# A two-layer decoder trunk: output-weight sums loaded ahead and stored in one go, the last two products exchanged, score groups joined

## The chip, the cores and the metric

The kernel runs on one core of one Trainium2 chip. The metric is the device time of one execution in microseconds, lower is better. Before the change the median of three executions is 1103.44 us (1101.58 to 1105.78). A profiled execution of its own took 1101.21 us; its span, from the first to the last instruction, is 1099.5 us.

## The reference

The input is 1024 tokens of 1024 float32 numbers. Two layers follow.

```python
# layer 1: gated MLP with a causal mixing of tokens inside chunks of 128
u, v, z = split(rms_norm(h) @ w_in, 3)            # 1024 x 2048 each
v = layer_norm(gelu(v))
s = einsum('gts,bnsgc->bntgc', tril(w_s), v) + b_s   # 8 groups of 256 channels
h = h + rms_norm((gelu(u) * s * silu(z)) @ w_out)
k, v = rms_norm(h) @ w_k, rms_norm(h) @ w_v          # 4 heads of 64, shared
# layer 2: attention over a window of 128 keys, 16 query heads, ALiBi, one sink per head
q, z = split(rms_norm(h) @ w_in, 2)
p = softmax([q k^T / 8 + alibi, sink])               # the sink only enters the sum
h = h + rms_norm((p v * silu(z)) @ w_out)
```

## The kernel before

Every large matrix product is done to nearly float32 precision in three matmuls. Each operand is split into a rounded part *hi* and a rest *lo* (`split`: ScalarE writes hi with a copy, L105, VectorE writes lo by a subtraction, L106), and `mm3` (L203 to L205) adds hi x hi, hi x lo and lo x hi into one bank. On top of this the products of a two-by-two block matrix are done in seven products in place of eight (the Winograd form of Strassen's scheme), numbered 1 to 7. It needs sums and differences of the blocks of either operand, and sums of the products.

The stages, in order: `v_layer` (v), `uz_layer` (u and z, the token mixing, the gate), `out_layer` (the first output product and its norm), query and gate products, keys and values, and attention, into which the remaining products are filled, ending with the output product of layer 2 (`Out.early`, `Out.late`).

**uz_layer** goes over 16 *quads*: eight channel groups g, each first for u (zz = 0), then for z (zz = 1). A quad does products 1, 2, 6, 5, 7 of its own and products 4 and 3 of the quad before. Products 1, 6 and 7 add into one bank (tile `ub` in the profile): after each, ScalarE copies the running sum out (`copy`, L243), and the next product adds on. Products 5 and 3 use the bank `uc`, product 2 uses `ua`. `prep1` to `prep3` make the split weights a product or two ahead (GpSimd makes the sums `f`, L240). Gelu (L724) and silu (L654) stand on ScalarE and each needs its function table loaded. `normalise` (L638) works on the group's part of v (`vg`), which `group_consts` loads; `spatial` does the mixing.

**presum** is a generator that uz_layer steps six times a quad (`step(sums_b)`). It has nothing to do with that stage: it makes the sums of the layer-2 output weights `wo_b` that the seven products at the end need, in 16 pieces of 128 columns, splits them, and stores hi and lo to DRAM (`od`). Piece by piece, before the change: four loads, five additions on GpSimd, four splits, eight stores, three splits, six stores. All seven blocks of a piece lie in one tile `presum`, of which the lo parts overwrite the sums, so the next piece's loads go into what the last piece's stores read.

**The order of the work.** The program is traced in Python's order, and a scheduler with a cost model then orders each engine's instructions by priority and by when it takes their inputs to be there. `tc.keep_in_program_order` pins an instruction behind the one traced last on its engine. On the chip each engine works off its list in order; DMAs that SyncE (SP) issues stand in one such list too, and each waits there for what it needs.

**Weights** (class `Weights`) hands out split weight pairs through `wnext`. The first 20 are split on the spot; later ones are read back from DRAM by `back`, among them the output weights in the order 4, 2, 5, 1, 7, 6, 3, two halves u each, into a ring of three pairs (`o_ring`).

**Attention** runs 16 units (a block of 128 queries and a pair of key heads). `ORDER` gives the parts of a step: 0 and 1 are the two score groups, a and b their exponentials, n and m their normalising, t the transposes of the unit before, v, g and p values, gate and split of the one before that, F a piece of the filling products. Scores, transposes and values share four banks with the tag "s". VectorE reduces the scores (L1134, L1141).

**The end.** `Out.early` does products 4, 2, 5, 1, 7 for 512 tokens in four blocks t; `final` (L1281) applies the root of the norm and adds the residual, and stores to the output (L1282). `Out.late` does product 6 into banks of its own and then product 3 (`og`), and adds the latter to two sums. Each block then has two squares on ScalarE (L1319), two scalings, the root on GpSimd (L1275) and two final passes.

## Time and profile before

| | before |
|---|---|
| median of three executions | 1103.44 us |
| profiled execution, its span | 1101.21 us, 1099.5 us |
| TensorE busy | 1043.5 us (95%) |
| VectorE, ScalarE, GpSimd busy | 780.2, 546.0, 266.0 us |
| mean granted TensorE clock | 0.975 |
| uz_layer, first to last product | about 162 to 541 us |

Columns of a row of the page: line, engine, operation, output tile and input tiles, sizes, count. PE is TensorE, PEld its weight loads, DVE VectorE, ACT ScalarE, POOL GpSimd, SPq the DMA list of SyncE. A timeline row has the start, the duration, and in brackets how long the engine was idle before it and who released it. Matmuls overlap: a row says 0.39 us, but they follow each other 0.227 us apart, so the distance of starts is what counts.

### The profile page before, as it was taken

The numbers are of one execution on the slowest core, as the hardware profiler recorded it, in microseconds if no ns is written. First come the engines' busy times: TensorE is split into PE (matmuls) and PEld (weight loads), VectorE is DVE, ScalarE is ACT, GpSimd is POOL, SyncE is SP. The second block draws the span as 40 slices with busy tenths as digits, with TensorE's granted clock in tenths as the row PEclk, the third lists the DMA queues.
The fourth block names the chain that finished last, engine by engine and source line by source line (L and its number), as shares of the span: only waits on it lengthen the run. The fifth ranks groups of instructions, "written<-read, shape, count | busy, mean of one in ns | idle before, by whom it ended". The sixth has DMA issues, their size and how long they took to land.

```text
span 1099.5 us, 15046 instructions
## 1 busy us (share of the span) xinstructions
PE 1043.5 (95%) x5186; PEld 848.7 (77%) x5186; DVE 780.2 (71%) x1374; ACT 546.0 (50%) x1046; POOL 266.0 (24%) x260
## 2 busy tenths in 40 slices
PE   9999999899889898899999999999999999998983
PEld 7887888787668687787888888888987777776772
DVE  6988377859667697867778668555166667778565
ACT  6684255555545556555444556444044445454322
POOL 0000023365353635353100000000001113144324
PEclk9999999999989999999999999999999999999896
DMA  8786245655545454555898652997145334344472
GB/s 305 261 284 251 96 153 159 182 161 164 157 154 154 142 168 152 171 160 173 300 358 309 232 181 89 325 350 249 58 159 194 137 135 145 124 148 156 170 270 110
DMA packets 130285, 210.17 MB, mean 191 GB/s; under 512 B 11681, under 2 KB 71969, under 8 KB 130209
## 3 DMA queue, kind: packets, MB, share of 16 engines
q1 hardware_dynamic: 125696, 200.53, 53.9%
q10 hardware_dynamic: 4512, 8.68, 2.2%
q8 instruction: 41, 0.67, 0.3%
q14 instruction: 36, 0.29, 0.1%
HBM read 144.15 MB, written 65.01 MB: 190 GB/s over the span
## 4 chain that ended last, share of the span: by engine, by line
PE 63%; DVE 13%; DMA 9%; POOL 6%; ACT 4%; issue 3%; SPq 2%; DVEq 0%; POOLq 0%; ACTq 0%
PE qz L203 6%; PE qz L204 5%; PE qz L205 5%; DVE uz_slots L240 4%; PE ob L205 3%; PE ob L203 3%; PE oc L203 3%; PE ob L204 3%; PE oc L204 3%; PE oc L205 3%; POOL presum L240 3%; PE vb L204 2%; PE vb L205 2%; DMA presum<-in_wo_b_dram 2%; DMA od<-presum 2%
## 5 line engine op out<-in xcount | busy, mean ns | idle before, releaser
L1147 ACT ACTIVATE pr<-pr,mx 128x129 f32<-128x129 f32 x128 | 50.4, 395 | 70.9 <-DVE mx L1141 70.9
L203 PE MATMUL ub<-T,uzhilo_g 128*128 128x512 f32 x128 | 55.6, 434 | 25.8 <-ACT uz_slots L243 25.8
L203 PE MATMUL qz<-n_hi,whi_w 128*128 128x512 f32 x192 | 77.4, 403 | 0.0
L204 PE MATMUL qz<-n_lo,whi_w 128*128 128x512 f32 x192 | 75.0, 391 | 0.0
L205 PE MATMUL qz<-n_hi,wlo_w 128*128 128x512 f32 x192 | 74.9, 390 | 0.0
L105 ACT ACTIVATE presum<-presum 128x128 fp32r<-128x128 f32 x112 | 31.4, 305 | 85.4 <-POOL presum L240 52.6
L106 DVE TENSOR_TENSOR presum<-presum 128x128 fp32r<-128x128 f32 x112 | 41.5, 408 | 42.4 <-POOL presum L240 34.5
L110 DVE SCALAR_TENSOR_TENSOR wlo_w<-raw_w,gn,whi_w 128x512 fp32r<-128x512 f32 x40 | 28.7, 748 | 48.4 <-ACT whi_w L109 48.4
L109 ACT ACTIVATE whi_w<-raw_w,gn 128x512 fp32r<-128x512 f32 x40 | 27.1, 716 | 62.9 <-PE pv L205 30.4
L203 PE MATMUL ub<-T,whi_g 128*128 128x512 f32 x128 | 51.9, 406 | 2.4 <-ACT uz_slots L243 2.4
L204 PE MATMUL ub<-T,uzhilo_g 128*128 128x512 f32 x128 | 53.4, 417 | 0.0
L205 PE MATMUL ub<-T,uzhilo_g 128*128 128x512 f32 x128 | 53.4, 417 | 0.0
L203 PEld LDWEIGHTS ub<-T,uzhilo_g 128*128 128x128 f32 x128 | 26.2, 204 | 34.4 <-ACT uz_slots L243 29.2
L1167 POOL TENSOR_SCALAR_AFFINE_SELECT pc<-pc 128x1024 f32<-128x1024 f32 x16 | 21.4, 1336 | 121.7 <-DVE dn L1153 109.6
L205 PE MATMUL ub<-T,wlo_g 128*128 128x512 f32 x128 | 50.7, 396 | 0.0
L204 PE MATMUL ub<-T,whi_g 128*128 128x512 f32 x128 | 50.6, 395 | 0.0
L240 POOL TENSOR_TENSOR presum<-presum 128x128 f32<-128x128 f32 x80 | 38.9, 517 | 46.9 <-DMA presum<-in_wo_b_dram 38.6
L106 DVE TENSOR_TENSOR uzhilo_g<-f,uzhilo_g 128x1024 fp32r<-128x1024 f32 x31 | 43.8, 1414 | 7.8 <-ACT uzhilo_g L105 7.3
L203 PE MATMUL uc<-T,uzhilo_g 128*128 128x512 f32 x124 | 48.9, 395 | 0.0
L204 PE MATMUL uc<-T,uzhilo_g 128*128 128x512 f32 x124 | 48.3, 389 | 0.0
L205 PE MATMUL uc<-T,uzhilo_g 128*128 128x512 f32 x124 | 48.3, 389 | 0.0
L240 POOL TENSOR_TENSOR f<-raw_uz 128x512 f32<-128x512 f32 x15 | 20.1, 1338 | 112.5 <-DMA raw_uz<-in_wuz_in_dram 96.3
(400 smaller groups left out, 3332.0 us busy)
## 6 DMA issues: line engine op xcount, KB each, us to landing
raw_uz<-in_wuz_in_dram SPq DMA_DIRECT2D x32, 512.0 KB, 3.9
od<-presum SPq DMA_DIRECT2D x224, 64.0 KB, 1.9
td<-uz_slots SPq DMA_DIRECT2D x56, 256.0 KB, 2.1
orawP2a<-td SPq DMA_DIRECT2D x28, 512.0 KB, 4.2
raw<-in_wv_in_dram SPq DMA_DIRECT2D x17, 512.0 KB, 4.7
vg<-vd SPq DMA_DIRECT2D x8, 1024.0 KB, 6.4
orawP2b<-in_wo_a_dram SPq DMA_DIRECT2D x16, 512.0 KB, 7.7
raw_w<-in_wqz_dram SPq DMA_DIRECT2D x16, 512.0 KB, 5.2
```

Source lines behind the costliest of these rows:

```text
L105: nc.scalar.activation(hi, src, AF.Copy)
L106: nc.vector.tensor_tensor(lo, src, hi.bitcast(F32), ALU.subtract)
L109: nc.scalar.activation(hi, src, AF.Copy, scale=g)
L110: nc.vector.scalar_tensor_tensor(lo, src, g, hi.bitcast(F32), ALU.mult, ALU.subtract)
L203: nc.tensor.matmul(out, lhsT=a_hi, rhs=b_hi, start=start, stop=False, skip_group_check=True)
L204: nc.tensor.matmul(out, lhsT=a_hi, rhs=b_lo, start=False, stop=False, skip_group_check=True)
L205: nc.tensor.matmul(out, lhsT=a_lo, rhs=b_hi, start=False, stop=stop, skip_group_check=True)
L240: (eng or nc.vector).tensor_tensor(out, a, b, op)
L1147: nc.scalar.activation(pr[:, i], pr[:, i], AF.Exp, bias=mx[:, i:i + 1], scale=-1.0, accum_out=dn[:, i:i + 1])
L1167: nc.gpsimd.affine_select(pc, pc, [[0, 8], [1, P]], ALU.is_ge, 0.0, base=0, channel_multiplier=-1)
```

## The change

- *presum*: a piece's four blocks come with two loads into a tile of their own (tag "junk"), and the loads of the next piece are put out right after the sums of this one. The five sums go from the raw blocks into five tiles `lo`, pinned in program order on GpSimd; five splits follow, pinned on ScalarE and VectorE; one DMA then stores all ten tiles. Blocks m = 4 and m = 3, which are plain blocks of the weights and no sums, are no longer made here.
- *Weights*: halves of m = 4 and m = 3 are loaded raw one pair ahead and split when their pair is fetched (`early_raw`, `back`). Product 3 now comes before product 6.
- *uz_layer*: `load_consts(g + 1)` moves behind `normalise(g)`, and the masking of `wc` on GpSimd becomes `mask_consts`, called in the z quad.
- *Attention*: `ORDER` has 0 and 1 next to each other. In the last four units the difference that product 3 needs stays where it is made and is what `post` splits; the sum for product 6 is split in `late`.
- *The end*: `late` does product 3 first and then product 6 on top of it in the same banks (after the block's sum with product 3 alone is read out). The second half's scaling goes to VectorE, into another tile; the root's first part is made for four blocks at once. The output stores of blocks 0 and 1 of the first half are put out after the last weights have been asked for.

```diff
-            self.order += [(None, f"o{m}{u}") for m in (4, 2, 5, 1, 7, 6, 3) for u in range(2)]
+            self.order += [({4: wo_b[1, u], 3: wo_b[0, 2 + u]}.get(m), f"o{m}{u}")
+                           for m in (4, 2, 5, 1, 7, 3, 6) for u in range(2)]
...
         def back(self, i):
             for n in range(20 + len(self.ready), i + 1):
                 self.ready[n] = (w_ring if n < 36 else o_ring).take(f"w{n}")
+                if self.order[n][0] is not None and n >= 36:
+                    self.early_raw(n)
+                    split(*self.ready[n], self.raw[n])
+                    continue
                 for t, src in zip(self.ready[n], self.kept[self.order[n][1]]):
                     nc.sync.dma_start(out=t.bitcast(F32), in_=src)
+            self.early_raw(i + 1)
+
+        def early_raw(self, n):
+            if 36 <= n < len(self.order) and self.order[n][0] is not None and self.raw.get(n) is None:
+                self.raw[n] = wload(self.order[n][0], f"w{n}")
...
+        def mask_consts(g):
+            wc = grp[g]["wc"]
             tc.keep_in_program_order(
                 nc.gpsimd.affine_select(wc, wc, [[1, P]], ALU.is_ge, 0.0, base=0, channel_multiplier=-1))
...
             else:
                 normalise(g)
+                if g + 1 < G:
+                    load_consts(g + 1)
...
     def presum(t):
-        made = ((4, 3), (2, 6), (5, 5), (1, 4), (7, 1), (6, 2), (3, 0))
+        lo = [t[:, i].bitcast(F32) for i in range(5)]
+
+        def fetch_four(n):
+            r = st.tile([P, 4, P], F32, tag="junk", name=f"presum_raw{n}", bufs=1)
+            for i in range(2):
+                src = wo_b[i].rearrange("(l u) p c -> u p l c", u=2)[n // 8]
+                load(r[:, 2 * i:2 * i + 2], src[:, :, n % 8 * P:n % 8 * P + P])
+            return [r[:, k] for k in range(4)]
+
+        raw = fetch_four(0)
+        yield
         for n in range(16):
             u, at = n // 8, slice(n % 8 * P, n % 8 * P + P)
-            for a, i, l in ((a21, 1, 1), (a22, 1, 0), (a11, 0, 1), (a12, 0, 0)):
-                load(a, wo_b[i, 2 * l + u][:, at])
+            a12, a11, a22, a21 = raw
+            m6, s1, s5, s2, m7 = lo
+            for o, a, b, op in ((s1, a11, a22, ALU.add), (s5, a11, a12, ALU.add), (m6, a21, a11, ALU.subtract),
+                                (m7, a12, a22, ALU.subtract), (s2, a21, a22, ALU.add)):
+                tc.keep_in_program_order(nc.gpsimd.tensor_tensor(o, a, b, op))
             yield
-            add(s1, a11, a22, ALU.add, nc.gpsimd)
...
+            if n < 15:
+                raw = fetch_four(n + 1)
             yield
-            for part in (made[:4], made[4:]):
-                for k, (m, i) in enumerate(part):
-                    split(t[:, 7 + k], t[:, i], raw[i])
-                yield
-                for k, (m, i) in enumerate(part):
-                    for e, x in enumerate((7 + k, i)):
-                        nc.sync.dma_start(out=od[f"o{m}{u}"][e][:, at], in_=t[:, x].bitcast(F32))
-                yield
+            yield
+            for k in range(5):
+                hi = t[:, 5 + k]
+                tc.keep_in_program_order(nc.scalar.activation(hi, lo[k], AF.Copy))
+                tc.keep_in_program_order(nc.vector.tensor_tensor(t[:, k], lo[k], hi.bitcast(F32), ALU.subtract))
+                if k == 2:
+                    yield
+            nc.sync.dma_start(out=od[u].rearrange("s p c -> p s c")[:, :, at], in_=t.bitcast(F32))
+            yield
+            yield
...
-                self.d, eng = yt, nc.gpsimd if t < 3 else nc.vector
+                self.d = e = z[0][:, :, (b % 4) * P:(b % 4 + 1) * P]
+                eng = nc.gpsimd if t < 3 else nc.vector
...
-    ORDER = "0Fav1FbgmtpFFn"
+    ORDER = "01FavFbgmtpFFn"
...
-                if t:
-                    final(*self.rest.pop(0))
+                if t in (1, 2):
+                    final(*self.rest.pop(0), self.stores)
...
+            for k, _ in enumerate(self.product(ps, self.of(q1, 1), True, False, after3)):
+                if k < 4:
+                    d = self.z[1][:, :, k * P:(k + 1) * P]
                     hi, lo = (by_head(w)[:, 0:2, k] for w in q1)
+                    split(hi, lo, d.rearrange("p (m g) t -> p m g t", m=2))
+                elif k == 4:
+                    w = [wnext() for _ in range(2)]
+                    for dst, src in self.stores:
+                        tc.keep_in_program_order(nc.sync.dma_start(out=dst, in_=src))
+                elif k == 5:
                     final(*self.rest.pop(0))
+                elif k == 6:
+                    hf = big.tile([P, 4, D], F32, tag="P0a", name="hf1")
+                    xt = [load(hf[:, t], h1d[1][t]) for t in range(4)]
+            final(*self.rest.pop(0))
...
-                    mm3(ps[t], a[0], a[1], hi[:, cs], lo[:, cs], m == 0, m == 3)
-                for i, c in enumerate((m5[t], n2[t])):
-                    add(c, c, ps[t], ALU.add)
-                    self.square(1, i, t, c)
-                c = m5[t]
-                add(c, c, gp[0], ALU.mult, nc.gpsimd if t < 3 else nc.vector)
-                r = final_rstd(1, t, self.ss[1])
-                c = n2[t]
-                add(c, c, gp[1], ALU.mult, nc.gpsimd)
+                    mm3(ps[t], a[0], a[1], hi[:, cs], lo[:, cs], False, m == 3)
+                c, o, r = n2[t], self.m4[t], ef[:, 4 + t:5 + t]
+                add(c, c, ps[t], ALU.add)
+                self.square(1, 1, t, c)
+                add(o, c, gp[1], ALU.mult)
                 if t:
                     final(*self.rest.pop(0))
+                nc.vector.tensor_scalar(r, self.ss[1][:, 1, t:t + 1], 1.0 / D, ef[:, t:t + 1], ALU.mult, ALU.add)
+                nc.gpsimd.tensor_tensor(r, r, nhalf[:, 0:1], ALU.pow)
```

More of the change, by code (lines that the diff above doesn't have):

```diff
@@ L152, in split @@
                 self.load(n)
-                raw, kind = self.raw[n], self.order[n][1]
-                if kind in self.kept:
+                raw, kind = self.raw.get(n), self.order[n][1]
+                if n >= 20:
                     self.back(n)
@@ L185, in gain @@
         return gn[:, c + k:c + k + 1]
-    od = {f"o{m}{u}": [dram.tile([P, 1024], F32, name=f"od{m}{u}_{i}") for i in range(2)]
-          for m in range(1, 8) for u in range(2)}
+    od = [dram.tile([10, P, 1024], F32, name=f"od{u}") for u in range(2)]
     w_pair = pair_of(wpool, "w", 2)
@@ L683, in uz_layer @@
         more = up.tile([P, 6, TH], F32, name="uz_slots")
-        sums_b = presum(up.tile([P, 11, P], F32R, name="presum"))
+        sums_b = presum(up.tile([P, 10, P], F32R, name="presum"))
         four = big.tile([P, 4, TH], F32, tag="P1_3", name="uz_slots4")
@@ L712, in uz_layer @@
             step(sums_b)
+            if live and zz and g + 1 < G:
+                mask_consts(g + 1)
             if q > 0:
@@ L766, in presum @@
     def presum(t):
-        raw = [t[:, i].bitcast(F32) for i in range(7)]
-        a11, a12, a21, a22, s1, s5, s2 = raw
-        yield from range(0)
-        made = ((4, 3), (2, 6), (5, 5), (1, 4), (7, 1), (6, 2), (3, 0))
+        lo = [t[:, i].bitcast(F32) for i in range(5)]
[5 more added lines that the diff above has]
+            return [r[:, k] for k in range(4)]
@@ L1276, in final_rstd, with final @@
         return r
-    def final(h, t, yo, r, xt):
+    def final(h, t, yo, r, xt, later=None):
         for i in range(2):
@@ L1281, in final @@
             nc.vector.scalar_tensor_tensor(yo[i], yo[i], r, xt[:, cs], ALU.mult, ALU.add)
-            (nc.scalar if (h, t, i) == (1, 3, 1) else nc.sync).dma_start(
-                out=out[h * TH + t * P:h * TH + (t + 1) * P, cs], in_=yo[i])
+            dst = out[h * TH + t * P:h * TH + (t + 1) * P, cs]
+            if later is not None:
+                later.append((dst, yo[i]))
+            else:
+                (nc.scalar if (h, t, i) == (1, 3, 1) else nc.sync).dma_start(out=dst, in_=yo[i])
     yd = [[dram.tile([P, 512], F32, name=f"yd{p}_{t}") for t in range(4)] for p in range(2)]
@@ L1343, in early @@
             gp = self.gp
-            self.rest, self.o = [], {}
+            self.rest, self.stores, self.o = [], [], {}
             own = [big.tile([P, n, 4, 512], F32, tag=tag, name=f"sum_{tag}")
```

46 lines of the change are left out of this document (19 added, 27 removed).

## The prediction

> **What bounds the kernel now.** I read the page first, then busy time by stage, then the waits of the one stage in which TensorE rests, then single stalls in the timeline.
>
> ```profile
> span 1099.5 us, 15046 instructions
> ...
> PE 1043.5 (95%) x5186; PEld 848.7 (77%) x5186; DVE 780.2 (71%) x1374; ACT 546.0 (50%) x1046; POOL 266.0 (24%) x260
> ...
> ```
>
> TensorE is busy for 95% of the span, so no change can bring more than the rests and the stretches at a lowered clock. The stage table shows where these are (columns: stretch, its length, busy time and count of PE, PEld, DVE, ACT, POOL, then the granted clock and DMA).
>
> ```profile
> 162.00:541.00 379.00, 350.81 (x1619) 290.38 (x1618) 289.30 (x475) 206.89 (x336) 164.73 (x174) 0.96 0.53 167
> 310.00:320.00 10.00, 5.59 (x23) 4.34 (x23) 6.55 (x12) 7.10 (x13) 5.21 (x7) 0.84 0.41 131
> 900.00:950.00 50.00, 50.00 (x327) 37.32 (x326) 41.60 (x123) 27.69 (x90) 13.43 (x11) 1.00 0.38 130
> 1000.00:1040.00 40.00, 34.89 (x186) 26.57 (x185) 29.19 (x64) 18.59 (x52) 15.84 (x13) 0.91 0.42 149
> ```
>
> The first row is the whole gate-and-value stage (uz_layer): 379.0 - 350.8 = 28.2 us of TensorE rest. The second row shows one of its stalls from near: 5.59 busy of 10, at 0.84 of the clock. Attention is full (50.00 of 50 in 900 to 950), its end is not (34.89 of 40, clock 0.91). The lowered clock costs the stage 0.04 x 350.8 = 14 us by the rounded mean of the first row; the same sum over its slices of ten us, of which the second row is one (0.16 x 5.59 = 0.9), gives 10.9, and I take this lower one. So about 39 us of this stage can be had.
>
> The waits of that stretch (who waited for whom: total us, times, longest):
>
> ```profile
> ACT presum L105 <- POOL presum L240: 52.6, 26, 4.9
> ...
> POOL presum L240 <- DMA presum<-in_wo_b_dram: 38.6, 11, 8.7
> DVE presum L106 <- POOL presum L240: 34.5, 12, 6.1
> ...
> PE ub L203 <- ACT uz_slots L243: 28.2, 10, 4.7
> ...
> ACT presum L105 <- DMA od<-presum: 19.4, 10, 5.2
> DVE vg L638 <- DMA vg<-vd: 13.7, 7, 3.0
> ```
>
> TensorE's 28.2 us are ten waits for one thing: ScalarE's copy of the bank (L243). ScalarE itself waited 52.6 + 19.4 us, and VectorE 34.5, at the splits of the output-weight sums (presum). These stand in in-order queues, so whatever is behind them waits too. One stall shows the chain:
>
> ```profile
> 314.34 0.39 PE L205 MATMUL uc<-T,uzhilo_g 128*128 128x512 f32 x1
> 319.14 0.79 PE L203 MATMUL ub<-T,uzhilo_g 128*128 128x512 f32 x1 [4.41 <-ACT uz_slots L243]
> 311.79 0.73 ACT L105 ACTIVATE presum<-presum 128x128 fp32r<-128x128 f32 x2 [2.70 <-POOL presum L240]
> 313.46 0.31 ACT L105 ACTIVATE presum<-presum 128x128 fp32r<-128x128 f32 x1 [0.94 <-POOL presum L240]
> ...
> 315.08 0.63 ACT L724 ACTIVATE uz_slots<-uz_slots 128x512 f32<-128x512 f32 x1
> 315.62 1.04 ACT L105 ACTIVATE uzhilo_g<-f 128x1024 fp32r<-128x1024 f32 x1
> 316.68 1.28 ACT L654 ACT_TABLE_LOAD   x1
> ...
> 318.51 0.58 ACT L243 ACTIVATE uz_slots<-ub 128x512 f32<-128x512 f32 x1
> 310.76 0.68 DVE L240 TENSOR_TENSOR uz_slots<-uz_slots,bc 128x512 f32<-128x512 f32 x1
> ```
>
> The product that runs to 314.34 + 0.39 = 314.73 (product 5, 12 matmuls 0.227 apart, 2.7 us) has the other bank, so product 6 had left its bank by 312.0 and it could have been copied under product 5. ScalarE instead waited 2.70 and 0.94 us for GpSimd's sums, and then had a table load, a gelu, a split, a second table load and a silu ahead of the copy. The copy came at 318.51, TensorE stood 4.41 us. GpSimd was late because its loads were (38.6 us), and these because a piece's loads go into tiles that the last piece's stores still read.
>
> **The change, part by part.** *Presum.* Per piece, four loads become two, put out a quad ahead into a tile of their own; fourteen stores become one of ten tiles; seven splits become five.
>
> ```profile
> L788 SPq DMA_DIRECT2D od<-presum x224: 319/382/1645, 173.5 to 502.2; - x112
> 162.00:541.00 379.00, 41.48 (x112) 31.43 (x112) 38.86 (x80) 0.96 0.53 167
> od<-presum SPq DMA_DIRECT2D x224, 64.0 KB, 1.9
> ...
> vg<-vd SPq DMA_DIRECT2D x8, 1024.0 KB, 6.4
> ```
>
> The first row is the issuing of the stores on SP, the second the busy time of the sums on VectorE, ScalarE and GpSimd in the stage, the last two give size and time to landing. So 208 stores of 0.38 us leave SP's queue (79 us of issuing, not TensorE's time), and 32 of 112 splits leave VectorE (32/112 x 41.48 = 12 us) and ScalarE (9 us). The sums no longer wait for a load that was put out one step before. The bundled store (640 KB in 512-byte rows) is not in the trace: its landing lies between the 1.9 us of a 64 KB store and the 6.4 us of the 1 MB of vg. I take 5, near vg, because of the size. It is issued at a quad's end, and the next sums stand three products later (36 x 0.227 = 8.2 us), so GpSimd should find it landed. Behind the sums on GpSimd stand the f sums and the group subtractions, which have their inputs later anyway.
>
> How much of the stall goes? In the one shown, without the two waits and the 0.7 us of splits between them, the gelu starts when VectorE's scaling (310.76 + 0.68) is there, about 311.4. Gelu, split, table load and silu then take up to the copy what they took before, 318.51 - 315.08 = 3.4 us: copy at 314.9, bank free at 315.5, against 319.1 and an ideal 314.56. About 0.9 us of 4.41 remain, four fifths go. But VectorE also waits 13.7 us for vg, which this change moves only indirectly, and is busy 289 of 379 us, so I take three quarters for the ten: 0.75 x (28.2 + 10.9) = **29.3 us**. Bounds: all (39), and below nothing (the rival on the other side).
>
> The clock part goes by the rows: 0.84 around this stall, and, below, matmuls of 0.79 us after rests of 2.25 and 0.93 us. The Trainium skill ("TensorE: Matmul & The Clock Gate", What's actually happening) has the clock halved after an idle window of about 3.4 us and for as long until it is released; by that, of ten stalls with a mean of 2.8 us, only the longest would cost clock (half of 3.4, 1.7 us each; for three of them 5 us in place of 10.9, an estimate from that page), and the presum term would be about 25. The trace shows a slow clock after shorter rests, so the row decides.
>
> *Group constants.* The loads of wc and bsb go from the quad's end to behind the normalising, and the mask on GpSimd a quad later. Nothing on the path waits for them; cover: a whole quad of seven products. Cost 0; without the cover, one landing (1.9 to 6.4 us by the rows above) in each of eight groups, in GpSimd's free time (164.7 busy of 379).
>
> *Output weights m 4 and 3 raw.* Four splits of 1024 columns (1.04 us on ScalarE at 315.62 above; on VectorE, which needs 0.68 for 512 columns in the row at 1090.82 below, some 1.3) move into the late attention. There TensorE is full, VectorE has 41.60 of 50 and ScalarE 27.69, and each split is issued a weight pair before it is needed. Cost 0; with no cover 4 x 1.3 = 5 us. They also save two 512 KB reads each for one.
>
> *Last two products.* Their weights come late now:
>
> ```profile
> 1062.43 0.33 SPq L1282 DMA_DIRECT2D out_dram<-sum_P2a  x1
> 1062.86 0.88 SPq L142 DMA_DIRECT2D wm_w<-od  x2
> 1067.32 0.47 PE L203 MATMUL og<-wm_w,q_hi 128*128 128x512 f32 x1 [2.25 <-DMA wm_w<-od]
> 1068.72 0.79 PE L204 MATMUL og<-wm_w,q_hi 128*128 128x512 f32 x1 [0.93 <-DMA wm_w<-od]
> ...
> 1081.81 0.39 PE L204 MATMUL og<-wlo_w,q_hi 128*128 128x512 f32 x1
> 1082.04 0.39 PE L205 MATMUL og<-whi_w,q_lo 128*128 128x512 f32 x1
> ```
>
> The load of the last weights stands on SP behind output stores, which wait for VectorE. The last product starts at 1067.32 after 2.25 us, waits 0.93 more, runs slow, and ends at 1082.43. Its 48 matmuls at 0.23 us (1081.81 to 1082.04) are 11.0 us; from the start of the wait, 1065.07, that would be 1076.1: 6.4 us lost. After the change the stores of the first two blocks go out behind the weight loads. The second pair of weights still needs the buffer that the first half of the product before frees, 5.5 us ahead of that product's end, about what such loads take. I take **5.5** (bounds 0 and 6.4).
>
> *The tail behind the last matmul.*
>
> ```profile
> 1088.56 1.74 DVE L1281 SCALAR_TENSOR_TENSOR sum_P2a<-sum_P2a,ef,hf 128x512 f32<-128x512 f32 x1
> ...
> 1090.82 0.68 DVE L240 TENSOR_TENSOR sum_P2a<-sum_P2a,og 128x512 f32<-128x512 f32 x1
> ...
> 1092.61 0.21 DVE L1274 TENSOR_SCALAR ef<-ssb,ef 128x1 f32<-128x1 f32 x1
> ...
> 1095.60 0.74 DVE L1281 SCALAR_TENSOR_TENSOR sum_P2a<-sum_P2a,ef,raw_hf 128x512 f32<-128x512 f32 x1
> 1090.99 0.63 ACT L1319 ACTIVATE junk_b<-sum_P2b 128x512 bf16<-128x512 f32 x1 [3.37 <-DVE sum_P2b L240]
> 1093.77 1.00 POOL L1275 TENSOR_TENSOR ef<-ef,small 128x1 f32<-128x1 f32 x1
> ```
>
> From 1082.43 to 1099.5 are 17.1 us: VectorE works off two to three blocks, each with two additions, two final passes (1.74 us beside a GpSimd multiplication, 0.74 alone), and two sums of squares on ScalarE ahead of the root. After the change products 3 and 6 share a bank, so a block has one addition, one square and one scaling behind the matmuls, all but the root on VectorE: 0.68 + 0.68 + 2 x 0.74 + 0.21 = 3.05 us against 48/4 x 0.227 = 2.7 of TensorE. At the last matmul VectorE is therefore about one final pass behind. From there: 0.2 handing over, 0.68 addition, 0.68 scaling, 1.5 final pass of block 2, 0.2 and 0.6 to 1.0 for the root, 1.5 final pass of block 3, then 1099.5 - (1095.60 + 0.74) = 3.2 for the store: 8.7 to 9.1. The square (0.63) runs under the scaling. Gain 17.1 - 9.0 = **8.1** (bounds 4, if GpSimd's other multiplications still slow these, and 8.5). What is new in the way: TensorE adds product 6 into a bank only after VectorE has read product 3 from it. The reading is three blocks (4.1 us) ahead; uncovered it costs one addition, 0.7.
>
> *Score groups joined.* Group 1 is put out straight after group 0, so all four small banks are taken, and the values of the unit before last reuse group 0's banks with only one fill step (6 matmuls, 1.4 us) between, where before a step and the values lay ahead of group 1's reuse. In return exponentials and transposes come earlier. From the chain of waits a score group and the values, and from the waits after 1000 what TensorE stood for:
>
> ```profile
> 924.18 0.84 PE s L1127 x12
> 926.61 1.45 PE o L1190 x16
> PE s L1127 <- DVE mx L1141: 4.1, 2, 2.2
> ```
>
> These two waits (4.1) and the clock of 0.91 (0.09 x 34.9 = 3.1) make 7.2 us at the end of attention, the most that joining can gain. The slack that is lost is values against score group, 1.45 - 0.84 = 0.6 us; if VectorE used all of it in each of 16 units, that is 10. VectorE's late queue causes the waits, and it is not shorter, so I take 0.
>
> **The sum.** 29.3 + 5.5 + 8.1 = 42.9. The profiled execution took 1101.2 us (span 1099.5 and 1.7 around it), 2.2 below the median of 1103.44. 1101.2 - 42.9 = 1058.3; from the median 1060.5. I predict 1060.
>
> **The rivals.**
> *VectorE takes over (24%).* It is busy 76% of the stage; with TensorE's stalls gone its load would be (289 - 11)/345 = 81%, and it has vg to wait for. If copies stay queued behind gelu, silu and table loads, a third of the stage's loss goes (13), and 10 of the end: 1080. For it: VectorE's wait for vg and the two table loads in the stall. Against it: the 34.5 us it stood for presum alone.
> *Everything goes (14%).* 39 + 6.4 + 8.5 + half of the 7.2: 1046, in the extreme 1042.
> *The loads are not led (8%).* A load a quad ahead waits on SP for the sums before it; if weights and vg queue behind it there, the stalls keep their size and only the end gains 13: 1090. Against it: 208 stores fewer in the same queue.
> *Slower (9%).* The one store needs all five splits, the next sums need the store, and the pinned splits cannot be passed on ScalarE and VectorE. If the store lands after the sums are due, every one of 16 pieces makes both queues wait. At the longest stall of today (4.7) plus 1.1 of clock (10.9 over ten), 16 x 5.8 = 93 us against 39 now, less 13.6 at the end: 1143. It turns slower where a piece costs TensorE over (39 + 13.6)/16 = 3.3 us. For it: ScalarE waits 19.4 us for landing stores already. Against it: 8.2 us of products against a landing of 5.
> The forecast itself has 45%, 1046 to 1074.
>
> Range 1042 to 1092: it takes in the first three rivals but for their edges, and leaves out the slower one. What this kernel's measurement can tell from no change is about 0.5%, 5.5 us; every case but the slower one is faster by more, at its middle; a little of that one and of the third rival may end inside. Faster 0.89, same 0.03, slower 0.08.
>
> **What would show it.** Right: TensorE's waits for L243 under 10 us in the stage, its clock above 0.98, hardly any waits at presum on ScalarE and VectorE, no wait for the last weights, 9 us behind the last matmul. Wrong: waits of GpSimd for od stores (the slow rival), waits for vg or uz_slots in their place (VectorE's), waits of the values for mx in attention (the joined groups), or the last product still waiting for its weights.

## The result, and the profile after

The changed kernel takes 1045.49 us (median of four executions, 1044.52 to 1045.90). The kernel before, run beside it on the same chip, takes 1102.74 us (1101.58 to 1105.78). The ratio is 0.9476 with a 95% interval from 0.9455 to 0.9497, 57 us less. The forecast was 1060, with a range of 1042 to 1092. The time lies in the range, near its fast edge, and half a us outside the 1046 to 1074 that the forecast gave itself.

From the page after: the span, the busy times, and the row of the bundled store (count, KB each, us to landing).

```profile
span 1042.8 us, 14527 instructions
...
PE 1025.3 (98%) x5186; PEld 839.6 (81%) x5186; DVE 792.4 (76%) x1342; ACT 541.1 (52%) x1018; POOL 276.2 (26%) x257
...
od<-presum SPq DMA_DIRECT2D x16, 640.0 KB, 4.0
```

VectorE and GpSimd are busy for longer than before (780.2 and 266.0 us), in a shorter span. The stages of the kernel after follow, in the columns of the stage table before. The gate-and-value stage now ends near 499 us and not near 541.

```profile
162.00:499.00 337.00, 336.06 (x1616) 282.35 (x1615) 301.65 (x436) 196.98 (x299) 179.12 (x174) 1.00 0.53 171
310.00:320.00 10.00, 10.00 (x54) 8.59 (x53) 8.46 (x13) 6.60 (x10) 5.63 (x8) 1.00 0.45 123
...
960.00:985.00 25.00, 20.88 (x106) 14.83 (x105) 19.82 (x46) 13.95 (x38) 9.58 (x9) 0.86 0.45 159
```

In the first row TensorE rests 337.0 - 336.06 = 0.9 us where it rested 28.2, at a mean clock of 1.00 where it had 0.96. The ten us from 310, which held a stall before, are full. The last row is a stretch that is still lossy, at the end of attention: 4.1 us of rest, and a clock of 0.86; the stretches beside it, 930 to 960 and 985 to 1012, are full. VectorE is busy for 301.65 of 337 us in the first row, 90%. The prediction had reckoned with 81%, and had made a rival of it.

Who waits for whom in that stretch (total us, times, longest):

```profile
POOL presum L803 <- DMA od<-presum: 84.8, 14, 10.0
ACT uz_slots L256 <- PE ub L218: 37.4, 16, 3.4
...
ACT presum L811 <- POOL presum L803: 2.9, 1, 2.9
```

Of ScalarE's 52.6 + 19.4 us at presum 2.9 are left, and of VectorE's 34.5 none. The copy of the bank (L256, formerly L243) now waits for TensorE, and the other way round only 0.9 us are left. The waiting has moved to GpSimd: 84.8 us for the landing of the one store. That is the sign that the prediction had given to the slow rival. Here it costs TensorE nothing that shows, the 0.9 us being all of its rest in the stage: GpSimd is busy 179 of 337 us, and what stands behind its wait is not yet due.

What TensorE itself waited for, over the whole span:

```profile
PE o L1218 <- DVE mx L1169: 4.1, 2, 3.0
...
PE ub L216 <- ACT uz_slots L256: 0.9, 2, 0.5
```

No wait for the last weights remains. The end, from the timeline after:

```profile
1011.56 0.39 PE L216 MATMUL of<-whi_w,q_hi 128*128 128x512 f32 x1
1033.10 0.39 PE L218 MATMUL of<-whi_w,q_lo 128*128 128x512 f32 x1
1011.76 0.80 SPq L150 DMA_DIRECT2D wm_w<-od  x2
...
1017.86 0.38 SPq L1439 DMA_DIRECT2D out_dram<-sum_P  x1
...
1039.00 0.75 DVE L1309 SCALAR_TENSOR_TENSOR sum_P<-sum_P,ef,hf 128x512 f32<-128x512 f32 x1
```

The loads of the last weights (1011.76) now go out ahead of the output stores (1017.86). The two products run without a gap, 21.9 us from 1011.56 to 1033.10 + 0.39; before, from the first of them to the last matmul's end, it was 28.4. From 1033.49 to the end of the span, 1042.8, are 9.3 us in place of 17.1, and the last final pass takes 0.75 us, as all of them do now; before, one beside a GpSimd multiplication took 1.74.

The gains of the two profiled executions, between first matmuls of the same products, add up to the difference of the spans (1099.5 - 1042.8 = 56.7):

| stretch | before | after | gain |
|---|---|---|---|
| gate and value stage, to the first `ob` | 378.5 | 337.1 | 41.4 |
| the last two products | 28.4 | 21.9 | 6.5 |
| behind the last matmul | 17.1 | 9.3 | 7.8 |
| all else | | | 1.0 |

### The profile page after: what moved, and what is told of

Same layout as the page of the kernel before. It is cut to its first block, busy times and chain, and to the rows that moved or that the text cites. A ratio compares the mean times of both kernels' runs of the same rounds, so it can differ in the third digit from the quotient of the medians.

```text
span 1042.8 us, 14527 instructions
## 1 busy us (share of the span) xinstructions
PE 1025.3 (98%) x5186; PEld 839.6 (81%) x5186; DVE 792.4 (76%) x1342; ACT 541.1 (52%) x1018; POOL 276.2 (26%) x257
## 4 chain that ended last, share of the span: by engine, by line
PE 74%; DVE 7%; DMA 7%; issue 5%; ACT 3%; POOL 2%; SPq 1%; POOLq 0%; DVEq 0%; ACTq 0%
PE qz L216 5%; PE ub L216 5%; PE ub L218 5%; PE ub L217 5%; PE qz L218 5%; PE qz L217 5%; PE sp L659 2%; PE uc L217 2%; PE uc L216 2%; PE uc L218 2%; PE o L1218 2%; PE s L1155 2%; PE ob L218 2%; PE ob L216 2%; PE ob L217 2%
## 5 line engine op out<-in xcount | busy, mean ns | idle before, releaser
L803 POOL TENSOR_TENSOR presum<-presum_raw 128x128 f32<-128x128 f32 x80 | 49.1, 645 | 91.9 <-DMA od<-presum 84.8
L216 PE MATMUL ub<-T,uzhilo_g 128*128 128x512 f32 x128 | 50.7, 396 | 0.9 <-ACT uz_slots L256 0.9
L106 DVE TENSOR_TENSOR uzhilo_g<-f,uzhilo_g 128x1024 fp32r<-128x1024 f32 x31 | 47.3, 1526 | 5.4 <-ACT uzhilo_g L105 5.4
L812 DVE TENSOR_TENSOR presum<-presum 128x128 fp32r<-128x128 f32 x80 | 50.6, 681 | 0.1
L218 PE MATMUL ub<-T,uzhilo_g 128*128 128x512 f32 x128 | 49.9, 390 | 0.0
L217 PE MATMUL ub<-T,uzhilo_g 128*128 128x512 f32 x128 | 49.9, 390 | 0.0
L105 ACT ACTIVATE uzhilo_g<-f 128x1024 fp32r<-128x1024 f32 x31 | 32.8, 1057 | 32.2 <-PE uc L218 25.9
L256 ACT ACTIVATE uz_slots<-ub 128x512 f32<-128x512 f32 x48 | 28.2, 587 | 39.7 <-PE ub L218 37.4
```

What stands on the lines that cost most here:

```text
L105: nc.scalar.activation(hi, src, AF.Copy)
L106: nc.vector.tensor_tensor(lo, src, hi.bitcast(F32), ALU.subtract)
L216: nc.tensor.matmul(out, lhsT=a_hi, rhs=b_hi, start=start, stop=False, skip_group_check=True)
L217: nc.tensor.matmul(out, lhsT=a_hi, rhs=b_lo, start=False, stop=False, skip_group_check=True)
L218: nc.tensor.matmul(out, lhsT=a_lo, rhs=b_hi, start=False, stop=stop, skip_group_check=True)
L256: nc.scalar.activation(out, a, AF.Copy)
```

## The experiments

The change is a bundle, and two questions stand behind the sum. Does it fall apart into the sums' part and the end's part? And which of the five things done to presum (loads led by a quad, a tile of their own for them, splits three steps behind the sums, pins, fewer splits and one store) makes the 41 us?

**The end alone.** The old kernel with the edits of `Out`, `final` and the order of products 3 and 6; presum, ORDER and the group constants as before.

```diff
-  for m in (4, 2, 5, 1, 7, 6, 3) for u in range(2)]
+  for m in (4, 2, 5, 1, 7, 3, 6) for u in range(2)]
...
```

> The kernel before with only the end changed: product 3 before product 6 in shared banks, its operand from the other tile, scaling on VectorE, output stores of blocks 0 and 1 put off. Sums of the output weights and score groups as before. If the parts add up as the two profiles read, this gains what the end shows there: 6.5 us from the start of the last two products to the last matmul, and 7.8 behind it, 14.3 in all: 1102.7 - 14.3 = 1088.4 us, and uz_layer keeps its 28 us of stalls. Rival: the end gained because the sums had changed too (four raw weight pairs, less on SP): then it gains less than 8 us, above 1094.

Measured: 1091.18 us, ratio 0.9909 (0.9884 to 0.9934), a gain of 9.7, between the two expectations. What TensorE waited for in it:

```profile
PE ub L203 <- ACT uz_slots L243: 27.4, 11, 4.9
...
PE qz L203 <- ACT whi_w L109: 1.6, 1, 1.6
PE od L203 <- DVE sum_P2a L240: 1.6, 1, 1.6
```

The end itself gained nearly what it gains in the whole change: 6.5 us in the last two products, 7.0 behind the last matmul. The stalls of the first stage are untouched. The profiled execution lost 6.9 us further up: 3.1 in the first stage and 3.8 between the first query product and the first keys, where it waits 1.6 us for `whi_w`. Up to there all engines work off the same instructions in the same order as in the kernel before, so another order is not the cause. That execution was the slowest of the four (1094.94 us), but the median, too, lacks some 4 of the 13.5 us, and why stays open.

**The sums alone.** The changed kernel with the old end, the old ORDER and product 6 ahead of 3.

> The other half: sums of the output weights, weights 4 and 3 loaded raw, group constants moved, with the end and the score groups of before (product 6, then 3). Parts that add up: 1102.7 - 41.4 = 1061.3 us, uz_layer from 378.5 to 337 us, and the last product still waits about 3 us for its weights. Rival: the last weights of before came late because of the many sums' stores or of pairs read back from DRAM; then the raw pair comes in time, the wait goes too, and the time is below 1056.

Measured: 1057.43 us, ratio 0.9599 (0.9581 to 0.9617), a gain of 43.5, again between the two expectations. The first `ob` comes at 498.1 us (498.7 in the whole change), and the last product still waits for its weights, 2.4 us for `whi_w`, as the first theory has it. So presum and what goes with it give about 41 of the 57 us. The rest is the end, which is 3.9 us shorter than before even with its old code, less small losses between. That 9.7 + 43.5 = 53.2 falls 4 short of 57 needs no part that only the whole change has: the end alone lost as much further up.

**Loads not led.** The changed kernel, with each piece's loads put out one step ahead of its sums, still into their own tile.

```diff
-        raw = fetch_four(0)
-        yield
         for n in range(16):
+            raw = fetch_four(n)
+            yield
...
-            if n < 15:
-                raw = fetch_four(n + 1)
...
-            yield
```

> The kernel after, but each piece of the sums is loaded one step ahead of its additions, as before, and not a quad ahead. Theory (what counts is that the splits stand far behind the additions, so that GpSimd takes up every wait): GpSimd waits 2 to 5 us more per piece, the splits three products later do not notice: within 3 us of 1045.5. Rival (the lead of the loads is what removed the stalls): GpSimd's sums come late as before, the splits on ScalarE and VectorE wait for them, stalls of 15 to 28 us and their clock return: 1065 to 1085.

Measured: 1046.39 us, ratio 0.9504 (0.9485 to 0.9523). It can't be told from the whole change: leading the loads by a quad is worth nothing that these runs can show. GpSimd still waits 83.5 us for the store, so a load that comes earlier only waits with it.

**Splits close behind the sums.** The two empty steps between sums and splits are moved behind the store.

```diff
-            yield
-            yield
             for k in range(5):
...
             yield
             yield
+            yield
+            yield
```

> The kernel after, but the five splits of a piece and its store come right behind the additions (the step after), as before, and not three steps later. Loads still led by a quad, one store, five splits, pinned. Theory (distance of the splits): ScalarE and VectorE wait for GpSimd's sums again, TensorE's stalls for the bank copy return at least by a third: above 1056. Rival (lead of the loads): the sums are early, so the splits find them: within 3 us of 1045.5.

Measured: 1085.32 us, ratio 0.9852 (0.9836 to 0.9867). The waits in the first stage:

```profile
ACT presum L809 <- POOL presum L803: 34.7, 9, 5.1
PE ub L216 <- ACT uz_slots L256: 24.1, 7, 5.4
```

The old chain is back: ScalarE stands at a split for GpSimd's sums, the copy of the bank stands behind it, TensorE rests. The distance is worth 40 us of what the whole has, about 36 in this stage and 6 in the one behind it. It is what lets GpSimd wait up to 10 us without TensorE noticing. With pins, the loads' own tile, two loads, five splits, one store, raw weights and moved group constants all in place, the stage is at 373.0 us to the first `ob`, against 378.5 before and 337.1 after: without the distance these bring 5.5 us between them.

**Ten stores in place of one.** Ten DMAs of 64 KB each, at the same place.

> The kernel after, with ten stores of 64 KB per piece in place of the one of 640 KB; all else as after. Theory (distance of the splits): 144 more issues on SP, about 55 us of its list, lie beside other work; GpSimd waits for stores a little longer; within 4 us of 1045. Rival (the short SP list is what removed the stalls): loads of weights and of vg come late, half of the stalls return, 1060 to 1070.

Measured: 1047.51 us, ratio 0.9501 (0.9477 to 0.9526). The bundling is worth nothing that these runs can show. GpSimd's wait for the stores is even shorter with the small ones (54.1 us against 84.8).

**No pins.** The three `keep_in_program_order` in presum are taken off; everything else stays.

> The kernel after, without the three pins in program order in the sums (GpSimd's additions, ScalarE's and VectorE's halves of the splits); the places in the program are the same. Theory in its first form (the place in the program gives the distance, the pins only hold it): the scheduler, which takes inputs to be there sooner than they are, moves the splits forward and half of the stalls return: 1055 to 1075. Rival (the distance in the program is enough): within 4 us of 1045.

Measured: 1080.39 us, ratio 0.9807 (0.9788 to 0.9826).

```profile
ACT presum L811 <- POOL presum L803: 59.5, 38, 5.7
...
PE ub L216 <- ACT uz_slots L256: 24.7, 7, 6.2
```

Left free, the scheduler puts the splits forward. In most pieces ScalarE's first split now stands right behind the first of the five sums, and ScalarE waits there 38 times. It also packs the pieces together. All sixteen are done by 336 us, in the changed kernel by 505, and TensorE's rest lies where they lie:

```profile
162.00:340.00 178.00, 153.28 (x673) 125.28 (x672) 124.00 (x238) 94.55 (x173) 92.85 (x121) 0.91 0.56 174
340.00:535.00 195.00, 195.00 (x946) 164.43 (x945) 142.86 (x204) 108.52 (x131) 72.18 (x54) 1.00 0.41 142
```

In this run the busy time of the presum tile's instructions alone in the stage, on VectorE, ScalarE and GpSimd, is

```profile
162.00:535.00 373.00, 27.22 (x80) 22.59 (x80) 40.62 (x80) 0.96 0.48 157
```

and the same row of the changed kernel has

```profile
162.00:499.00 337.00, 50.14 (x78) 18.64 (x78) 49.11 (x80) 1.00 0.53 171
```

27.22 us of VectorE stand against 50.14. VectorE works nearly twice as long at the same splits in the faster kernel. Busy time was no measure of the loss here; which instruction stands ahead of the copy was.

**Seven splits.** The changed kernel with two more splits per piece, into a spare tile; their results are not used.

> The kernel after, with two more splits per piece into a spare tile (their results are not used), so that ScalarE and VectorE do seven as before. Theory (not the work but the waiting was the cost): VectorE has 9 to 12 us more in uz_layer, and as it is busy for 90% of that stage already, some of it may show: 1045 to 1050. Rival (the shorter list of splits made the room): 1055 or more.

Measured: 1059.31 us, ratio 0.9612 (0.9594 to 0.9629), 13.8 us more than the whole change. Its stage table has

```profile
162.00:507.50 345.50, 337.96 (x1617) 281.84 (x1616) 314.01 (x466) 200.04 (x330) 184.59 (x174) 1.00 0.51 165
```

TensorE rests 345.5 - 337.96 = 7.5 us. The first `ob` comes 8.8 us later than after, and the stage behind it takes about 6 us longer, with one wait of 4.1 us for ScalarE's split of `ohiloP0a`. VectorE is at 314.01 of 345.5, 91%, and ScalarE's waits for it at `uz_slots` (gelu and silu) grow from 26.8 + 18.0 us to 45.4 + 39.3. With everything else in place the stage has no room for 32 more pairs of splits, so dropping blocks 4 and 3 from the list, which the prediction had booked as saved work beside the path, is a part of the gain.

**Distance and pins alone.** The old kernel (one tile, four loads, seven splits, fourteen stores) with its splits two steps later and pinned.

```diff
+            yield
+            yield
...
-                    split(t[:, 7 + k], t[:, i], raw[i])
-                yield
+                    tc.keep_in_program_order(nc.scalar.activation(t[:, 7 + k], raw[i], AF.Copy))
+                    tc.keep_in_program_order(
+                        nc.vector.tensor_tensor(t[:, i], raw[i], t[:, 7 + k].bitcast(F32), ALU.subtract))
```

> The kernel before with one thing changed: the seven splits of a piece stand two steps further behind the additions (at the fifth and sixth step of a quad) and are pinned in program order. Still four loads one step ahead, into tiles the stores read, fourteen stores, seven splits, old end, old score groups. Theory (distance and pins are the whole of it): uz_layer falls from 378 to below 350 us, the time to 1060 to 1075. Rival (it takes the loads, the one store and the shorter list together): the additions come a quad late because loads wait for the stores of the piece before, the splits still wait, and less than 10 us is won: above 1091.

Measured: 1127.14 us, ratio 1.0229 (1.0209 to 1.0249): slower than before by 24.

```profile
POOL presum L240 <- DMA presum<-in_wo_b_dram: 130.0, 14, 14.7
PE ub L203 <- ACT uz_slots L243: 45.8, 8, 7.9
...
ACT presum L786 <- POOL presum L240: 37.3, 15, 4.6
...
ACT presum L786 <- DMA od<-presum: 31.3, 8, 5.7
```

This is the slow rival of the prediction, on the chip: pinned splits that wait. The first and third rows show one loop: the next loads go into the tile that the stores read, so a longer way from sums to stores makes loads late, and sums, and splits. The fourth shows ScalarE waiting for a store directly. The last three splits of a piece write hi into slots that its first stores still read; the changed kernel has a slot for each.

**The shared tile put back.** The kernel with loads not led (1046.39), and its loads into four slots of the tile that the one store reads.

```diff
-            r = st.tile([P, 4, P], F32, tag="junk", name=f"presum_raw{n}", bufs=1)
+            r = t[:, 5:9].bitcast(F32)
```

> The changed kernel with the loads one step ahead of the sums (1046.4 as measured), and the loads no longer into a tile of their own but into four slots of the tile that the one store reads; distance, pins, five splits and one store per piece stay. The theory that the tile of its own is a necessary part expects what splits moved later and pinned in the old kernel gave, less the end (14) and the shorter list of splits (14): 1127 - 28 = about 1099, at least 1080, with TensorE's waits for the bank copy (L256) over 20 us and GpSimd's for the loads back over 80. The rival that distance, pins, the shorter list and the one store are enough expects 1046 to 1052: a store (4.0 us to landing) and a load (2.2) fit into the two steps of some 5 us between them, and what does not fit GpSimd takes up ahead of the three steps to the splits.

Measured: 1063.52 us, ratio 0.9628 (0.9592 to 0.9664), 17 more than with the own tile.

```profile
POOL presum L803 <- DMA presum<-in_wo_b_dram: 134.6, 16, 12.9
...
ACT presum L809 <- POOL presum L803: 24.7, 17, 9.0
...
PE ub L216 <- ACT uz_slots L256: 15.5, 8, 3.8
```

Both expectations missed. The own tile is needed, but for 17 us and not for 53. GpSimd waits as long for the loads as with distance and pins alone, yet ScalarE less for GpSimd, and not at all for stores. The run with distance and pins alone is slower by 1127.1 - 1063.5 = 63.6 us; the end (some 14) and the two pairs of splits (14) leave about 36, which I can't share out between the fourteen stores, the split slots that are used twice, the four loads and the sums that overwrite their inputs: no run has one of them alone.

**The old order of the score groups.** Only `ORDER = "0Fav1FbgmtpFFn"`.

> The changed kernel (1045.5) with the old order of the late attention's steps: score group 1 is put out one fill step after group 0, not straight after it. The theory that joining the groups was worth nothing expects within 2 us of 1045.5, and that the 4.1 us of TensorE's wait for mx before the last units goes back from the values to the scores. The rival that it is where the 4 us come from by which the end alone and the sums alone fall short of the whole change (9.7 + 43.5 = 53.2 against 57.2) expects about 1049.5, with the time between the first out-projection and the first of the last products longer by that.

Measured: 1047.07 us (1044.96 to 1047.88), ratio 0.9484 (0.9463 to 0.9504), not to be told from the whole change. TensorE's waits at the end of attention:

```profile
PE s L1155 <- DVE mx L1169: 2.5, 2, 1.9
PE od L216 <- DVE sum_P2a L253: 1.6, 1, 1.6
```

The wait goes back from the values to the scores, and again adds up to 4.1 with its neighbour. From the first `pk` to the first `of` it is 289.1 us against 286.5, so joining is worth 2.6 us at most in these two executions.

**The late splits pinned.** The same remedy at the one place that still stalls: the eight pairs of splits in `Out.sums` are pinned where the program has them. They split sums of the first operand for products 1 and 7; the expectation below wrongly calls them splits of the raw weights m 4 and 3. In the changed kernel VectorE works off seven of them from 966 to 971 us, ahead of the score reductions that TensorE then waits for.

```diff
-  split(*(self.o[m][:, e, t].rearrange("p m t -> p (m t)") for e in range(2)), raw[m, t])
+  hi, lo = (self.o[m][:, e, t].rearrange("p m t -> p (m t)") for e in range(2))
+  tc.keep_in_program_order(nc.scalar.activation(hi, raw[m, t], AF.Copy))
+  tc.keep_in_program_order(nc.vector.tensor_tensor(lo, raw[m, t], hi.bitcast(F32), ALU.subtract))
```

> The changed kernel (1045.5) with the splits of the raw m 4 and 3 output weights, in the late attention, kept where the program has them. The theory that scheduled splits which move forward make VectorE late holds that the same thing is behind the remaining 4.1 us wait of the values for mx before the last unit (VectorE works off splits from 963 to 971 us, ahead of that unit's score reduction): 4.1 us of waits and some 3 us of slow clock go, 1038 to 1042. The rival that the wait comes from the score reductions themselves, or that the splits then stand in the way a unit later, expects no change, 1044 to 1047, with the wait at another place.

Measured: 1043.37 us (1039.48 to 1048.17, six executions), ratio 0.9457 (0.9433 to 0.9482). The median is 2 us below the changed kernel's, and the intervals overlap: a version that may be better, not one that is shown to be. Its profiled execution was the slowest of the six. Its waits of TensorE from 930 us on:

```profile
PE pt L1189 <- DVE pr L1182: 2.1, 1, 2.1
PE o L1218 <- DVE mx L1169: 0.8, 1, 0.8
```

and two rows of its stage table:

```profile
960.00:985.00 25.00, 24.25 (x146) 17.71 (x145) 24.29 (x63) 17.77 (x57) 10.81 (x9) 1.00 0.37 121
985.00:1012.00 27.00, 24.90 (x125) 18.28 (x124) 18.38 (x26) 8.85 (x15) 6.39 (x5) 0.94 0.63 232
```

The wait for mx falls from 4.1 to 0.8 and the clock of its stretch comes back from 0.86 to 1.00, as the theory has it. But a wait of 2.1 us turns up one stretch later, at the transposes, where the pinned splits now stand beside the last normalising. From the first `pk` to the first `of` it is 283.6 us against 286.5. Both theories were half right.

**The last scaling back on GpSimd.** One argument, `nc.gpsimd`, in `Out.late`.

> The changed kernel (1045.5) with the last scaling of the sums put back on GpSimd. The theory that the stretch behind the last matmul got short because VectorE's final passes no longer run beside a GpSimd multiplication (1.74 us against 0.74) expects that stretch to be 2 to 5 us longer than 9.3 and the whole 1047 to 1050. The rival that the swap of the last products into shared banks (one addition, one square and one scaling per block) made all of it expects no change, 1044.5 to 1046.5.

Measured: 1048.16 us (1046.89 to 1049.79), ratio 0.9501 (0.9476 to 0.9525). Its last matmul and the last final passes of VectorE:

```profile
1034.93 0.39 PE L218 MATMUL of<-whi_w,q_lo 128*128 128x512 f32 x1
...
1038.52 1.82 DVE L1309 SCALAR_TENSOR_TENSOR sum_P2b<-sum_P2b,ef,hf 128x512 f32<-128x512 f32 x1
1040.26 0.74 DVE L1309 SCALAR_TENSOR_TENSOR sum_P<-sum_P,ef,hf 128x512 f32<-128x512 f32 x1
```

The pass beside the multiplication takes 1.82 us again. Behind the last matmul are 10.9 us, 1.6 more than after, just under what was expected. The other 6 of the 7.8 us come from the rest of the new end (shared banks with one addition, square and scaling a block, and the root's first part made for four blocks at once), which no run takes apart.

## Why the prediction was right, and where it was off

*What bounds the kernel* was read rightly. The ten waits for L243 and the slow clock beside them were the loss, ScalarE's queue was the way to it, and the change took it away.

*Presum* is the term that was mis-sized: 29.3 predicted, 41.4 measured, more even than the 39 that was to be its upper bound, and this is nearly the whole miss. Two choices made it small. First, of the two sums for the clock I took the lower, 10.9; measured, the rest fell by 27.3, so 41.4 - 27.3 = 14.1 was clock, as the rounded mean had said (14); TensorE's busy time in the stage fell by as much for the same products, 350.81 - 336.06 = 14.8. Second, I took three quarters of it. In the one stall worked out 0.9 us was to remain because gelu, table load and silu stayed ahead of the copy. They did not stay late: 0.9 us remain in the whole stage. The rival "everything goes" had the outcome (1046), at 14%; the forecast's own 45% went to slower times.

*The reason* was right in its chain and wrong in its remedy. The prediction held that the sums come in time because their loads do. The sums do not come in time for the place where the splits stood: with the splits close behind them ScalarE waits 34.7 us for GpSimd. The splits were moved so far back, and pinned there, that the lateness is used up before a queue that matters meets it. Undone one at a time (differences of the medians above), the pins are worth 35 us, the distance 40, the loads' own tile 17 and the two dropped pairs of splits 14; the lead and the bundling nothing. They add up to more than 41 because each is needed for the others. The runs were taken at several times and on two chips; by the ratios to the kernel before that ran beside each, the four come to 36, 41, 14 and 15 us, and the lead and the bundling to 3 each, inside the intervals. The step that failed beside the size is the one that let GpSimd find the store landed, 5 us inside 8.2 us of products: it lands in 4.0, and GpSimd still waits 84.8/14 = 6.1 us for it each time. The trace has no such cover. One piece:

```profile
204.55 0.49 DVE L812 TENSOR_TENSOR presum<-presum 128x128 fp32r<-128x128 f32 x2
205.09 0.39 SPq L815 DMA_DIRECT2D od<-presum  x1
209.24 2.71 POOL L803 TENSOR_TENSOR presum<-presum_raw 128x128 f32<-128x128 f32 x5 [9.27 <-DMA od<-presum]
```

GpSimd's list does not keep step with TensorE's products: it is at the sums 5.1 us before the last split lets the store go out, and the store then needs 4.0 to land. All fifteen times the sums begin within 0.2 us of the landing. Of the 91.9 us that GpSimd stands there (the 84.8, and 7.1 at one piece that the view puts down to VectorE), 36.6 lie before the store is put out, and the rest is its landing. The step was wrong, and that it did no harm is owed to the distance behind it.

*The slow rival* got its mechanism and its sign, but not here. Its condition, splits that wait while pinned, holds in the run with distance and pins alone, which is slower than before.

*VectorE takes over*: it came to 90% of the stage, far above the 81% of that rival, and TensorE did not wait for it. The rival read busy time where the order of the queue decides. Its core is right in one respect: two more splits a piece cost 14 us.

*The clock.* The granted clock rose with the rests gone, 0.96 to 1.00. The sum by the Trainium skill's idle window ("TensorE: Matmul & The Clock Gate", What's actually happening), 25 for the presum term, was further off than the one by rows. In the run with the late splits pinned a single rest of 2.1 us was followed by a slow clock, 0.57 from 989 to 992 us: eight transposes took 1.94 us after it, and 1.03 when it had not rested, 8.6 us earlier. That rest is shorter than the Trainium skill's window of about 3.4, so here the two differ and the measurement decides.

```profile
980.86 1.03 PE L1189 MATMUL pt<-ident,pr 128*128 128x128 f32 x8
...
989.46 1.94 PE L1189 MATMUL pt<-ident,pr 128*128 128x128 f32 x8 [2.10 <-DVE pr L1182]
```

*The last two products*: 5.5 predicted, 6.5 measured. I had held back 0.9 for the second pair of weights, and there was no wait for it. *The tail*: 8.1 predicted, 7.8 measured; 9.0 and 9.3 us behind the last matmul. (The prediction's terms for the latter add up to 8.6 to 9.0, not 8.7 to 9.1, which changes nothing.) *Group constants and raw weights*: no wait for either shows in the rows of TensorE. *Score groups joined*: 0 predicted. The wait of 4.1 us changed its name, to the values as foretold, and not its size, and the order alone can't be told from nothing.

## What to carry to other kernels

When side work shares in-order queues with the path, look for its instruction that waits ahead of an instruction the path needs, and move that one so far behind its producer that the producer's worst lateness fits in between; let the wait stand on the engine with room. A distance holds only if the scheduler can't shorten it (a pin) and if no buffer closes a loop from the late end back to the start. Price a term by what the whole stage loses, rest and clock; an engine's busy share is no verdict, since here the faster kernel had VectorE busier at the same work.

## What the runs showed that I had not expected

The splits of presum (128 x 128, on VectorE) take 50.14 us for 78 of them in the changed kernel, 643 ns each, and 27.22 for 80 without pins, 340 ns each, though the instruction is the same. Taken one by one, 51 of the 80 in the changed kernel last 0.28 to 0.30 us and 29 last 1.37 to 1.39. Each of the 29 began while a GpSimd instruction on 128 x 512 numbers was running, 0.1 to 0.5 us into it, and each ended 0.15 us after that instruction did. Two of them, and their neighbours:

```profile
263.08 1.74 POOL L253 TENSOR_TENSOR uz_slots<-uz_slots,uz_slots 128x512 f32<-128x512 f32 x1
263.59 2.68 DVE L812 TENSOR_TENSOR presum<-presum 128x128 fp32r<-128x128 f32 x2
264.78 1.34 POOL L253 TENSOR_TENSOR f<-raw_uz 128x512 f32<-128x512 f32 x1
```

Of the 51 short ones, 45 have no GpSimd instruction beside them, and six began a few ns ahead of theirs. So in these runs a split that begins second waits the other one out. Without pins less is lost because 14 of the 18 long splits stand beside presum's own sums of 128 x 128, which are over sooner: 0.54 to 0.62 us. A final pass at the end of the kernel is slower beside GpSimd, too: 1.82 us beside a multiplication, 0.74 alone.

And sixteen stores of 640 KB and 160 of 64 KB made no difference to the time that the runs can show, while GpSimd's wait for them differed by 30 us: a wait costs nothing as long as what stands behind it is not yet due.
